# Two transformer blocks in one launch: the low half of every second early weight unit made by an accumulating transfer

## The chip, the cores and the metric

One Trainium2 chip, one core. The metric is the device time of one execution in microseconds (us); lower is better. TensorE multiplies, VectorE (DVE) and ScalarE (ACT) do elementwise work, GpSimd (POOL) does a little of it, SyncE (SP) issues the loads.

## The reference

The reference runs a block of a first model (a hybrid mixer, cross attention to a memory, a gated feed-forward) and then two layers of a second one, on one sequence of 512 positions and width 1024, in float32. What matters here is its beginning:

```python
h = x
hn = rmsnorm(h, norm_mix_g[l])
h = h + hybrid_mixer(hn, w_in[l], ...)            # z = hn @ w_in; three branches; concat @ w_out
hn = rmsnorm(h, norm_x_g[l])
mn = rmsnorm(mem, norm_mem_g[l])                  # 256 rows of memory
h = h + cross_attention(hn, mn, w_xq[l], w_xkv[l], w_xo[l])
```

`hybrid_mixer` projects `hn` by `w_in`, and has a spatially gated branch, a branch with a causal depthwise convolution of 31 taps, and a chunkwise mLSTM branch of four heads, each with its own q, k and v weights.

## The kernel before, in words

**Products.** TensorE multiplies in a float32 form of reduced precision (`fp32r`). Each operand is therefore split into a high half (rounded to that form) and a low half (the rest), and `mm` (from line 597) makes each product of three matmuls: high by high, high by low, low by high.

**Weights.** They come in units of 128 partitions by 1024 float32 values (512 KB). `wunit` (line 630) takes a raw tile `wr` (three buffers), a page `wh` for the high half and one `wl` for the low one, issues the load on SP's queue, and splits the unit in two column halves of 512. For each, `split` (line 614) has ACT copy the raw values into `wh` and VectorE subtract: `wl = wr - wh`. The unit of a head's q, k and v weights is 384 wide and has one such half.

**Order.** Nothing runs when the code calls it. Engine calls are recorded as steps by `Recorder`; `Plan` gives each a price (`price1` and `price`, lines 150 and 203, with the delay until another engine sees the result), computes priorities, and simulates list scheduling (`run`) with limited buffers; `improve` repeats this with priorities from the last plan, eight times, and keeps the plan that is shortest by its own prices. `emit` then issues all steps in the planned order, so that each engine works through a fixed sequence, with waits only where data or buffers demand them. All of these instructions carry the line of `emit`'s call, L509, in the profile; the rows are told apart by their tiles. Three more rules matter:

- A unit's load waits until the unit `quota` places earlier (5 here) has been used up, and for a free raw tile. A load without predecessors may be planned at most 60 us of TensorE work ahead.
- Where the plan leaves TensorE idle for over 1 us, `emit` fills the gap with matmuls of the identity against itself (`ps<-ident`), in a number fixed by the plan.
- A tile is free, in the plan, when its last step has ended.

**The first stages.** `mix` (line 861) makes 20 units: in the order of the code, four of `w_in` each for the mLSTM input, the convolution branch, the gated branch and the output gate, and four units of q, k, v weights. `mem` (line 1225) has eight units of `w_xkv` for the keys and eight for the values, and `w_out` has eight. Units of `mix` and the keys are used by `proj_t` or a loop like it (24 matmuls a unit; 512 columns wide for the mixer, 256 for the keys). The convolution's 31 taps for each of two channel blocks (`taps`, tiles `gcv`) run on VectorE, as do normalisations by many tiny steps (`sm`). Cross attention (`xattn`) and all that follows come after `w_out`.

Of the kernel before, what the change touches and what calls it, by code (L numbers as in the profile page):

```python
# [7 lines left out]
F32 = mybir.dt.float32  # L8
# [3 lines left out]
AF = mybir.ActivationFunctionType  # L12
OP = mybir.AluOpType
# [76 lines left out]
class Engine:  # L90
    def __init__(self, rec, name):
        self.rec, self.name = rec, name
# [5 lines left out]
class Recorder:  # L98
# [10 lines left out]
    def add(self, forms, bias=0.0):  # L109

        if self.held is not None:
            self.held += forms[0]
            return
        o = Op()
        o.i = len(self.ops)
        o.reads, o.writes, o.keep = [], [], self.keep
        for eng, method, args, kw in forms[0]:
            outs = [kw["out"] if "out" in kw else args[0]]
            if kw.get("accum_out") is not None:
                outs.append(kw["accum_out"])  # L120
            ins = [x for x in (args if "out" in kw else args[1:]) if is_ap(x)]
            ins += [x for k, x in kw.items() if k not in ("out", "accum_out") and is_ap(x)]
            for x in outs + ins:
                if on_chip(x):
                    self.tiles[x.tensor.name] = x.tensor
            o.writes += [region(x) for x in outs if on_chip(x)]
            o.reads += [region(x) for x in ins if on_chip(x)]
        o.forms = [(f[0][0], f) + price(f) + (bias if f[0][0] == "vector" else 0.0, port(f)) for f in forms]
        self.ops.append(o)
        return o  # L130
# [19 lines left out]
def price1(eng, m, args, kw):  # L150
    out = kw["out"] if "out" in kw else args[0]
    ins = [x for x in list(args[1:]) + [x for k, x in kw.items() if k not in ("out", "accum_out")] if is_ap(x)]
    n = width(out)
    if m == "dma_start":
        return n * 4 * int(out.shape[0]) / 360e3 * (1 if run(out) >= 128 else 2)
    if eng == "tensor":
        if m == "transpose":
            return 0.109
        if "float32r" in str(args[1].dtype):
            return max(n / 2285.0 + 0.007, width(args[1]) / 1200.0 + 0.0025)  # L160
        return 4 * max(n, 64) / 2400.0
    ps = any("PSUM" in str(x.space) for x in ins + [out])
    if eng == "scalar":
        aps = sum(1 for k in ("scale", "bias") if is_ap(kw.get(k)))
        return (0.052 if ps else 0.094) + n / 1200.0 + 0.093 * (aps + (kw.get("accum_out") is not None))
    if eng == "vector":
        if m in ("bn_stats", "tensor_reduce"):
            return 0.065 + width(ins[0]) / 960.0
        if m == "bn_aggr":
            return 0.075  # L170
        cols = sum(1 for x in ins[1:] if int(x.shape[-1]) == 1 and n > 1)
        if m in ("tensor_scalar", "tensor_copy"):
            if ps:
                return 0.125 + n / 960.0
            return 0.06 + n / 1920.0 + (0.065 * max(1, cols) if m == "tensor_scalar" else 0)
        if m == "scalar_tensor_tensor":
            return (0.13 if cols or ps else 0.065) + n / 960.0
        if m == "memset":
            return 0.05 + n / 1920.0
        return 0.068 + n / 960.0  # L180
    if m in ("memset", "affine_select"):
        return 0.1 + n / 1200.0
    if m == "tensor_scalar":
        return 0.22 + n / 960.0
    return 0.15 + n / 476.0
# [17 lines left out]
def price(calls):  # L203

    t = sum(price1(*c) for c in calls)
    eng = calls[0][0]
    return t, {"tensor": 0.22, "scalar": 0.16, "vector": 0.12, "gpsimd": 0.12, "sync": 0.9}[eng]


# [323 lines left out]
class Block:  # L533
    def __init__(self, ctx, tc, a, out):
        self.tc, self.a, self.out = tc, a, out
        self.nc = Recorder(tc.nc)
        self.n = 0
        E = ctx.enter_context
        self.const = E(tc.tile_pool(name="const", bufs=1))
        self.wp = E(tc.tile_pool(name="wp", bufs=N_RAW))  # L540
        self.pgp = E(tc.tile_pool(name="pgp", bufs=N_PAGE))
        self.s2p = E(tc.tile_pool(name="s2p", bufs=N_HALF))
        self.small = E(tc.tile_pool(name="small", bufs=1))
        self.psp = E(tc.tile_pool(name="psp", bufs=8, space=PSUM))
        self.rules(5)
        self.early = 0
        self.x = self.const.tile([P, NT, D], F32, name="x")

    def uid(self, s):
# [80 lines left out]
    def wunit(self, loads, n=1024):  # L630

        nc = self.nc
        raw = self.wp.tile([P, 1024], F32, tag="wr", name=self.uid("wr"))
        hi, lo = self.page("wh"), self.page("wl")
        firsts = []
        for view, src in loads:
            firsts.append(len(nc.ops))
            nc.sync.dma_start(view(raw), src)
        nc.units.append((firsts, hi.tensor.name, self.quota))
        for c in ((0, 512), (512, n)) if n > 512 else ((0, n),):  # L640
            self.split(hi[:, c[0]:c[1]], lo[:, c[0]:c[1]], raw[:, c[0]:c[1]], weights=True)
        return Split(hi, lo)

    def unit_t(self, w, c0):
# [215 lines left out]

    def mix(self):
        nc, a = self.nc, self.a
        col = self.cols
        w_in = a["w_in"][0]
        self.rules(5)
# [11 lines left out]
        for c in range(2):  # L877
            hi, lo, src = gu[:, :, 32 * c:32 * c + 4], gu[:, :, 64 + 32 * c:68 + 32 * c], gw[:, :, 4 * c:4 * c + 4]
# [383 lines left out]

    def xattn(self, xT, kT, vv):
        nc, a = self.nc, self.a
        w_q = a["w_xq"][0]
        self.rules(6)
        self.early = 5
        oT = []
        for h in range(4):
            q = []  # L1270
            for j in range(2):
                ps = self.proj_t(self.unit_t(w_q, (2 * h + j) * P), xT)
                q.append(self.pair("q"))
                self.split(q[j].hi, q[j].lo, ps, 1.0 / 16.0)
            pT = self.duo("pT")
            for i2 in range(2):
                ps = self.ps()
                for ii in range(2):
                    i = i2 * 2 + ii
                    for j in range(2):  # L1280
                        self.mm(ps[:, ii * 256:(ii + 1) * 256], q[j][:, i * P:(i + 1) * P], kT[2 * h + j],
                                j == 0, j == 1)
                nm = self.sm([P, 2])
                nc.vector.tensor_reduce(nm, ps.rearrange("p (h m) -> p h m", m=256), axis=AX.X, op=OP.max,
                                        negate=True)
                p = self.s2("p")
                sm = self.sm([P, 2])
                for ii in range(2):
                    c = slice(ii * 256, (ii + 1) * 256)
                    nc.scalar.activation(p[:, c], ps[:, c], AF.Exp, bias=nm[:, ii:ii + 1], accum_out=sm[:, ii:ii + 1])  # L1290
                nc.vector.reciprocal(sm, sm)
                for ii in range(2):
                    c = slice(ii * 256, (ii + 1) * 256)
                    nc.vector.tensor_scalar(p[:, c], p[:, c], sm[:, ii:ii + 1], None, op0=OP.mult)
                pt = self.ps()
                self.turn(pt, [p[:, ii * 256 + c * P:ii * 256 + (c + 1) * P] for c in range(2) for ii in range(2)])
                o = pT.both[:, :, i2 * 256:(i2 + 1) * 256]
                self.split(o.hi, o.lo, pt.rearrange("p (c t) -> p c t", t=256))
            for j in range(2):
                b = 2 * h + j  # L1300
                ps = self.ps()
                for m in range(2):
                    self.mm(ps, vv[m][b // 4][:, (b % 4) * P:(b % 4 + 1) * P], pT.blocks[m], m == 0, m == 1)
                o = self.pair("o")
                self.split(o.hi, o.lo, ps)
                oT.append(o)
            if h == 1:
                self.proj_n(oT, a["w_xo"][0], 0)
        return self.proj_n_steps(oT[4:], a["w_xo"][0], 512)
# [585 lines left out]
```

## Time and profile before

| | us |
|---|---|
| median of 3 runs | 1964.94 (1964.29 to 1970.25) |
| the profiled execution, its own time | 1964.42 |
| its span, first to last instruction | 1962.6 |
| granted TensorE clock, mean | 0.994 |

The profile is of one execution. A row of the page's groups gives the engine, the operation, out<-in by tile names, count, busy time, mean duration and the idle time of the engine just before. Engines pipeline, so a row's mean can exceed the distance between two such instructions. Times of the timeline and of the chain are counted from the start of the span.

### The profile page before, as it was taken

The numbers are of one execution on the slowest core, as the hardware profiler recorded it, in microseconds if no ns is written. First come the engines' busy times: TensorE is split into PE (matmuls) and PEld (weight loads), VectorE is DVE, ScalarE is ACT, GpSimd is POOL, SyncE is SP. The second block draws the span as 40 slices with busy tenths as digits, with TensorE's granted clock in tenths as the row PEclk, the third lists the DMA queues.
The fourth block names the chain that finished last, engine by engine and source line by source line (L and its number), as shares of the span: only waits on it lengthen the run. The fifth ranks groups of instructions, "written<-read, shape, count | busy, mean of one in ns | idle before, by whom it ended". The sixth has DMA issues, their size and how long they took to land.

```text
span 1962.6 us, 26913 instructions
## 1 busy us (share of the span) xinstructions
PE 1930.5 (98%) x10348; PEld 1645.3 (84%) x10348; DVE 1214.9 (62%) x2690; ACT 824.2 (42%) x1673; POOL 78.5 (4%) x123
## 2 busy tenths in 40 slices
PE   9999999999999999999999999999999999999998
PEld 8888889798888878988788888778998988888776
DVE  5999665565434457688884345347686775344356
ACT  5476534344322333576534233233575434223330
POOL 0021000000000000012200000000000000000001
PEclk9999999999999999999999999999999999999999
DMA  6222423323222433510332233243223322233241
GB/s 172 80 69 65 155 87 103 97 65 118 65 76 75 118 108 83 110 32 22 99 106 76 75 108 97 75 127 104 76 76 97 98 76 91 67 98 105 70 150 43
DMA packets 215466, 177.38 MB, mean 90 GB/s; under 512 B 25174, under 2 KB 194202, under 8 KB 215338
## 3 DMA queue, kind: packets, MB, share of 16 engines
q1 hardware_dynamic: 215338, 175.66, 30.6%
q8 instruction: 81, 1.33, 0.3%
q14 instruction: 47, 0.39, 0.1%
HBM read 173.54 MB, written 2.10 MB: 89 GB/s over the span
## 4 chain that ended last, share of the span: by engine, by line
PE 86%; DVE 9%; ACT 3%; DMA 2%; issue 1%; SPq 0%; POOL 0%; DVEq 0%; ACTq 0%
PE ps L509 86%; DVE wl L509 2%; DVE sm L509 1%; DVE gcv L509 1%; ACT wh L509 1%; ACT p L509 1%; DMA wr<-in_mlp_w_dram 1%; DVE xtl L509 0%; DVE x L509 0%; DVE pt L509 0%; DMA wr<-in_w_up_dram 0%; ACT xth L509 0%; DMA g<-in_norm_mix_g_dram 0%; DMA wr<-in_w_down_dram 0%; DMA wr<-in_a_w_out_dram 0%
## 5 line engine op out<-in xcount | busy, mean ns | idle before, releaser
L509 ACT ACTIVATE wh<-wr 128x512 fp32r<-128x512 f32 x625 | 357.1, 623 | 423.5 <-PE ps L509 271.5
L509 DVE TENSOR_TENSOR wl<-wr,wh 128x512 fp32r<-128x512 f32 x625 | 406.2, 686 | 205.6 <-PE ps L509 96.8
L509 PE MATMUL ps<-xth,wh 128*128 128x512 f32 (+1 forms) x1464 | 516.9, 353 | 0.4 <-ACT hg L509 0.4
L509 PE MATMUL ps<-xtl,wh 128*128 128x512 f32 (+1 forms) x1464 | 514.4, 351 | 1.4 <-DVE xtl L509 1.4
L509 PE MATMUL ps<-xth,wl 128*128 128x512 f32 (+1 forms) x1464 | 513.4, 351 | 0.0
L509 PE MATMUL ps<-wh,hid 128*128 128x512 f32 (+1 forms) x1392 | 436.4, 391 | 1.8 <-ACT wh L509 1.7
L509 PEld LDWEIGHTS ps<-wh,hid 128*128 128x128 f32 x1392 | 260.3, 188 | 61.6 <-ACT wh L509 3.3
L509 PEld LDWEIGHTS ps<-xtl,wh 128*128 128x128 f32 x1464 | 276.2, 189 | 41.4 <-DVE xtl L509 2.6
L509 PEld LDWEIGHTS ps<-xth,wh 128*128 128x128 f32 x1464 | 276.4, 189 | 40.2 <-ACT xth L509 0.8
L509 PEld LDWEIGHTS ps<-xth,wl 128*128 128x128 f32 x1464 | 275.7, 188 | 39.9 <-DVE wl L509 0.2
L509 PE MATMUL ps<-wl,hid 128*128 128x512 f32 (+1 forms) x696 | 272.4, 391 | 1.6 <-DVE wl L509 1.5
L509 DVE TENSOR_TENSOR x<-x,ps 128x512 f32<-128x512 f32 (+1 forms) x210 | 141.1, 678 | 162.8 <-PE ps L509 162.2
L509 PEld LDWEIGHTS ps<-wl,hid 128*128 128x128 f32 x696 | 130.8, 188 | 34.2 <-DVE wl L509 4.8
L509 DVE TENSOR_TENSOR r<-r 128x512 f32<-128x512 f32 x62 | 42.8, 691 | 99.8 <-ACT r L509 99.7
L509 PE MATMUL ps<-wl,xth 128*128 128x256 f32 (+2 forms) x320 | 94.4, 295 | 3.4 <-DVE wl L509 3.4
L509 PE MATMUL ps<-wh,xth 128*128 128x256 f32 (+2 forms) x320 | 94.7, 296 | 0.0
L509 PE MATMUL ps<-wh,xtl 128*128 128x256 f32 (+2 forms) x320 | 93.9, 293 | 0.0
L509 ACT ACTIVATE r<-ps 128x512 f32<-128x512 f32 x64 | 38.0, 593 | 114.9 <-PE ps L509 114.9
L509 DVE SCALAR_TENSOR_TENSOR cv<-ps,cols,cv 128x511 f32<-128x511 f32 (+2 forms) x56 | 41.8, 746 | 39.1 <-ACT cv L509 38.5
L509 PEld LDWEIGHTS ps<-wl,xth 128*128 128x128 f32 x320 | 60.4, 189 | 5.6 <-DVE wl L509 4.2
L509 PE MATMUL ps<-wh,o 128*128 128x512 f32 x192 | 62.3, 394 | 0.0
L509 PEld LDWEIGHTS ps<-wh,xth 128*128 128x128 f32 x320 | 60.3, 189 | 1.4
(352 smaller groups left out, 2438.9 us busy)
## 6 DMA issues: line engine op xcount, KB each, us to landing
wr<-in_mlp_w_dram SPq DMA_DIRECT2D x128, 512.0 KB, 4.2
wr<-in_w_up_dram SPq DMA_DIRECT2D x44, 512.0 KB, 3.9
wr<-in_c_w_in_dram SPq DMA_DIRECT2D x24, 512.0 KB, 3.8
wr<-in_w_down_dram SPq DMA_DIRECT2D x22, 512.0 KB, 3.6
wr<-in_w_in_dram SPq DMA_DIRECT2D x16, 512.0 KB, 4.3
wr<-in_w_xkv_dram SPq DMA_DIRECT2D x16, 512.0 KB, 3.8
wr<-in_w_out_dram SPq DMA_DIRECT2D x8, 512.0 KB, 4.5
wr<-in_w_xq_dram SPq DMA_DIRECT2D x8, 512.0 KB
```

The lines of the kernel that those rows point to most:

```text
L509: getattr(getattr(self.rec.nc, eng), method)(*args, **kw)
```

## The change

In the mixer, the memory projection and `w_out` (`self.adding` is on from `mix` until `xattn`), every second unit, by the count of units made so far, gets its low half in another way. ACT still copies raw into the high half; ACT then copies the high half, negated, into the low half; and once both column halves are so filled, one transfer issued on GpSimd's queue adds the raw tile onto the low half in place (`accum_op=OP.add`). VectorE's subtractions of those units are gone. The planner gets a price for such a transfer: 1.2 us on GpSimd's queue, and 3.5 us more until another engine sees the result.

```diff
@@ price
     t = sum(price1(*c) for c in calls)
     eng = calls[0][0]
+    if eng == "gpsimd" and calls[0][1] == "dma_start":
+        return 1.2, 3.5
     return t, {"tensor": 0.22, "scalar": 0.16, "vector": 0.12, "gpsimd": 0.12, "sync": 0.9}[eng]
@@ Block.__init__
         self.early = 0
+        self.adding = False
@@ Block.wunit
         nc.units.append((firsts, hi.tensor.name, self.quota))
+        add = self.adding and len(nc.units) % 2 == 0
         for c in ((0, 512), (512, n)) if n > 512 else ((0, n),):
-            self.split(hi[:, c[0]:c[1]], lo[:, c[0]:c[1]], raw[:, c[0]:c[1]], weights=True)
+            c = slice(*c)
+            if add:
+                nc.scalar.activation(hi[:, c], raw[:, c], AF.Copy)
+                nc.scalar.activation(lo[:, c], hi[:, c].bitcast(F32), AF.Copy, scale=-1.0)
+            else:
+                self.split(hi[:, c], lo[:, c], raw[:, c], weights=True)
+        if add:
+            nc.gpsimd.dma_start(out=lo[:, :n], in_=raw[:, :n], accum_op=OP.add)
         return Split(hi, lo)
@@ Block.mix
+        self.adding = True
@@ Block.xattn
+        self.adding = False
```

## Rows read from the trace of the kernel before

**Rows 1.** the page: its busy line, and the share of each engine in the chain that ended last.

```profile
PE 1930.5 (98%) x10348; PEld 1645.3 (84%) x10348; DVE 1214.9 (62%) x2690; ACT 824.2 (42%) x1673; POOL 78.5 (4%) x123
...
PE 86%; DVE 9%; ACT 3%; DMA 2%; issue 1%; SPq 0%; POOL 0%; DVEq 0%; ACTq 0%
```

**Rows 2.** busy time of each engine in six of the eight stretches up to 283 us (the columns are in the first line; in brackets the instructions).

```profile
core 0: us, PE busy (x) PEld busy (x) DVE busy (x) ACT busy (x) POOL busy (x), PEclk, DMA share, GB/s
...
10.90:28.70 17.80, 17.73 (x131) 16.14 (x130) 17.75 (x54) 14.18 (x36) 0.69 (x2) 1.00 0.81 206
...
47.50:123.00 75.50, 74.26 (x366) 60.89 (x365) 73.03 (x140) 41.62 (x71) 5.76 (x12) 1.00 0.26 76
123.00:144.50 21.50, 21.40 (x109) 18.32 (x110) 21.16 (x68) 16.82 (x34) 4.49 (x7) 0.92 0.19 50
144.50:163.60 19.10, 17.58 (x92) 14.54 (x91) 16.67 (x85) 8.73 (x19) 3.56 (x6) 0.91 0.29 83
163.60:195.50 31.90, 31.86 (x190) 27.96 (x191) 30.87 (x136) 23.01 (x44) 4.42 (x4) 1.00 0.22 67
195.50:283.00 87.50, 87.50 (x469) 74.72 (x468) 54.91 (x133) 35.91 (x75) 0.00 (x0) 1.00 0.38 121
```

**Rows 3.** TensorE: the costliest groups between 47.5 and 195.5 us by line (count, busy us, mean ns, idle before), and one piece of its timeline (start us, us, what).

```profile
L509 PE MATMUL ps<-ident 128*128 128x512 f32 x141 | 35.1, 406 | 0.0
L509 PE MATMUL ps<-xth,wh 128*128 128x512 f32 x56 | 22.9, 409 | 0.4 <-ACT hg L509 0.4
...
80.20 15.94 PE L509 MATMUL ps<-ident 128*128 128x512 f32 x69
```

**Rows 4.** the chain that ended last, in order of time (start us, us, what).

```profile
20.66 0.76 DVE nat L509
21.46 49.43 PE ps L509 x340
70.92 0.60 ACT xc L509
...
84.36 4.53 DVE gcv L509 x7
...
123.10 21.41 PE ps L509 x107
...
145.07 0.74 DVE pw L509 x2
...
163.64 119.28 PE ps L509 x654
```

**Rows 5.** the page's group of the low weight halves (count, busy us, mean ns, idle before).

```profile
L509 DVE TENSOR_TENSOR wl<-wr,wh 128x512 fp32r<-128x512 f32 x625 | 406.2, 686 | 205.6 <-PE ps L509 96.8
```

**Rows 6.** VectorE's timeline: pairs of low halves.

```profile
77.82 1.28 DVE L509 TENSOR_TENSOR wl<-wr,wh 128x512 fp32r<-128x512 f32 x2
...
117.02 2.39 DVE L509 TENSOR_TENSOR wl<-wr,wh 128x512 fp32r<-128x512 f32 x2
```

**Rows 7.** the same stretches for the instructions that write or read `wl` alone (engines TensorE, its weight loads, VectorE).

```profile
47.50:123.00 75.50, 25.38 (x67) 12.41 (x66) 11.25 (x16) 1.00 0.26 76
123.00:144.50 21.50, 8.43 (x22) 4.48 (x22) 3.17 (x5) 0.92 0.19 50
144.50:163.60 19.10, 4.15 (x12) 2.26 (x12) 2.63 (x4) 0.91 0.29 83
163.60:195.50 31.90, 8.64 (x27) 5.10 (x27) 3.82 (x6) 1.00 0.22 67
195.50:283.00 87.50, 51.00 (x144) 26.95 (x143) 25.83 (x40) 1.00 0.38 121
```

**Rows 8.** VectorE's timeline before the first weights are used.

```profile
17.31 0.69 DVE L509 TENSOR_TENSOR wl<-wr,wh 128x512 fp32r<-128x512 f32 x1
...
19.72 0.68 DVE L509 TENSOR_TENSOR wl<-wr,wh 128x512 fp32r<-128x512 f32 x1
```

**Rows 9.** ScalarE's timeline: a pair of high halves.

```profile
54.40 1.15 ACT L509 ACTIVATE wh<-wr 128x512 fp32r<-128x512 f32 x2
```

**Rows 10.** transfers: from issue to landing of all loads into `wr`, and two kinds of load up to 300 us (count, KB each, median us to landing).

```profile
DMA to landing us min/median/max: 3.1/4.0/9.6
...
wr<-in_w_in_dram SPq DMA_DIRECT2D x16, 512.0 KB, 4.3
...
wr<-in_w_q_c_dram SPq DMA_DIRECT2D x4, 64.0 KB, 3.6
```

**Rows 11.** GpSimd's timeline: the subtraction beside the slow pair of rows 6.

```profile
117.51 1.35 POOL L509 TENSOR_TENSOR pl<-pw,ph 128x512 fp32r<-128x512 f32 x1 [1.28 <-ACT ph L509]
```

**Rows 12.** SP's queue: what it waited for up to 300 us, two loads of the key projection (one lies between them), and issue to landing of the loads from 180 to 256 us.

```profile
SPq L509 <- DVE wl L509: 185.3, 40, 19.1
...
197.50 0.34 SPq L509 DMA_DIRECT2D wr<-in_w_xkv_dram  x1
...
203.18 0.33 SPq L509 DMA_DIRECT2D wr<-in_w_xkv_dram  x1
...
DMA to landing us min/median/max: 3.7/3.9/4.5
```

**Rows 13.** TensorE's timeline near the dip of the granted clock (a bracket is idle time before, and its releaser).

```profile
120.73 0.39 PE L509 MATMUL ps<-v,ph 128*128 128x258 f32 x1 [0.54 <-DVE pw L509]
...
125.93 0.63 PE L509 MATMUL ps<-xth,wl 128*128 128x512 f32 x1
```

## The prediction, made before the changed kernel was run

> **What bounds the kernel now.** I began with the busy line and the chain over the whole span: TensorE is busy 98% of it and carries 86% of the chain that ended last, VectorE 9% [rows 1]. That says little about the edit, because TensorE's share holds filler. The change touches only the mixer, the memory projection and `w_out`, so the table by stretch comes next. It is cut where the chain changes hands, up to 283 us, where `w_out` is done [rows 2]. From 195.5 to 283 us VectorE has room (busy 54.91 of 87.5 us). From 47.5 to 195.5 us it has next to none: 73.03 of 75.5, 21.16 of 21.5, 16.67 of 19.1 and 30.87 of 31.9 us. TensorE looks full there too, but the lines of that stretch show 141 matmuls of `ident` against itself, the planner's filler, in runs such as 69 in 15.94 us, or 0.23 us apiece: some 32 us without real work [rows 3]. The chain in order of time agrees: from 70.92 to 123.10 us it is VectorE with short gaps, and again from 145.07 to 155.29 us, mostly the convolution's taps (`gcv`) and small statistics, with weight halves (`wl`) between them [rows 4]. After 163.64 us it reads as TensorE, but filler is part of that. So in this stage the end is set by VectorE's backlog, and every VectorE microsecond taken out before 195.5 us can become less filler. After 283 us nothing is edited, and I count no change there.
>
> **What leaves VectorE.** Every second unit counted in the order of the code: ten of the mixer's 20 (three are the narrow `qkv` ones), eight of the memory's 16, four of `w_out`'s eight, 22 in all. A half of 128x512 costs VectorE 0.686 us as a mean [rows 5], and two in a row take 1.28 us [rows 6], so about 0.60 us each when packed; all 22 units are 41 subtractions, some 24 us. Only those in the bound stretch count. The table of `wl` by stretch gives 16, 5, 4 and 6 between 47.5 and 195.5 us, 31 together [rows 7]. Half of them are 15.5, times 0.60 us = 9.3 us. The 40 from 195.5 us on are worth nothing: TensorE runs there almost without filler and covers them. Before 28.7 us VectorE is also full (17.75 of 17.8 us [rows 2]); the four halves at 17.31 to 20.32 us stand on the way to the last `nat`, after which TensorE starts on the weights at 21.46 us [rows 4, 8]. Unit 2 is one of these two units, so 2 x 0.60 = 1.2 us. Gain: 10.5 us.
>
> **What ACT takes on.** A negated copy per half; two copies `wh<-wr` take 1.15 us [rows 9]. The mixer's ten units and the memory's first three make 23 copies, some 13 us over the whole front, and 15.5 x 0.52 = 8 us inside the bound stretch, where ACT is busy 41.62 + 16.82 + 8.73 + 23.01 = 90.2 of 148 us [rows 2]. It rises to about two thirds, and I cost it at nothing while ACT has such gaps. Where it is ahead of an `xth` or `hg` on ACT's queue, TensorE already waits 0.4 us once [rows 3]; with the cover gone at all 23 that would be 9 us, which belongs to the wide end of the range.
>
> **What the transfer costs.** GpSimd issues no transfer in this trace, so its time T, from the start on that queue to the landing, is bounded. Below: the fastest weight load, 3.1 us from issue to landing. Above: the slowest, 9.6 us [rows 10]. Size hardly matters in these rows: 64 KB lands in 3.6 us and 512 KB in 4.3 us, so the bytes themselves are about 0.7 us of it. The new transfer reads a second stream, which I price as another 0.7 us, and its issue on GpSimd at 1.35 us, the longest single GpSimd subtraction [rows 11]: T = 4.0 (the median) + 0.7 + 1.35 = 6.0 us. This is nearest to an ordinary load, because it is one with more on it. The planner's new price, 1.2 + 3.5 us, is below that by 1.3 us. The plan also calls the raw tile free 1.2 us after the issue, although it is being read until the landing.
>
> The DMA page of the Trainium skill (DMA: Bandwidth & Descriptors, Anatomy of one DMA) fits a GpSimd-issued transfer as 2.0 us plus bytes over 436 GB/s; with the destination read too that would be an estimated 4.4 us here, and the loss of the next paragraph would be nought.
>
> **Where lateness bites.** There are three raw tiles, and SP's queue waited 185.3 us for `wl` to give them back [rows 12]. While keys are projected, loads follow each other by 2.84 us (two of them lie 5.68 us apart, from 197.50 us [rows 12]); that I take for TensorE's pace of one unit, since TensorE is busy throughout [rows 2]. An ordinary raw tile needs 3.9 us to land [rows 12], 1.2 for the copies and 0.6 for the trailing subtraction, 5.7 us; a new one 3.9 + 1.2 + 1.2 + T = 6.3 + T. Three tiles pass two units in (12.0 + T)/3 us, one in 2.0 + T/6. At T = 6.0 this is 3.0 us, 0.16 over that pace. Of the 16 units some five are prefetched (the quota), so 11 x 0.16 = 1.8 us is lost. At T = 3.1 it is nothing; at 9.6 it is 11 x 0.76 = 8.4 us. Queued behind a waiting load on SP are only later loads; behind a waiting transfer on GpSimd are the mask selects of `pw` and the `pl` subtractions, whose reader is TensorE. In the mixer a unit on TensorE takes 24 matmuls at 0.23 us = 5.5 us, so units are read well ahead and I cost lateness there at nothing; uncovered, each of its ten would add up to T. `w_out`'s units also last 5.5 us each and stay covered.
>
> **Sum.** -9.3 - 1.2 + 1.8 = -8.7 us on the profiled execution's own 1964.42 us (span 1962.6 us and 1.8 us around it): 1955.7 us. The median of the runs, 1964.94 us, stands 0.5 us above that execution, so 1956.2 us.
>
> **Rivals.**
> *The relief is absorbed.* All orders come out of a list planner that runs afresh, and VectorE's long chains (31 taps for each of two blocks, normalisations in series) need not get shorter when the gaps between them do. For it: the chain holds 21.41 us of TensorE in mid-stretch [rows 4]. Against it: VectorE has no idle time to speak of there. Then the gain is 0 to 5 us: about 1962 us.
> *Raw tiles are held too long.* The point is the key and value projection from 197.5 us. Break-even with 10.5 us of gain is 11 x (T/6 - 0.84) = 10.5, that is T = 10.8 us; if ACT's copies delay TensorE by 5 us, T = 8 us is enough. At T = 14 us it loses 16.4 - 10.5 = 6 us: 1971 us. A stall of TensorE is dearer than its length: after gaps like that at 120.73 us [rows 13] the granted clock of 123 to 163.6 us was 0.91 to 0.92 [rows 2], and a matmul of 512 columns took 0.63 us against a mean of 0.41 [rows 3, 13]: for part of it the clock was at 1.2 in place of 2.4 GHz.
> *The transfer starves beside VectorE.* At 117.02 us a `wl` pair took 2.39 us in place of 1.28 while GpSimd subtracted [rows 6, 11], so the two engines do block each other. If the making of a transfer's descriptors on GpSimd waits likewise for VectorE, which does not rest, each of the 13 early transfers gains several such 1.1 us, T passes 10 us, and TensorE waits in the mixer: 13 x 2 - 10.5 is 15.5 us slower, some 1980 us. For it: the collision. Against it: it has been seen with both engines reading.
> The SBUF page of the Trainium skill (SBUF — State Buffer, Who interferes with whom) says a GpSimd-issued transfer starves under VectorE's two-port forms (copies, `tensor_scalar`), and infers that `tensor_tensor` spares it; by this the rival would be confined to a few small operations, and no run here shows it yet.
> *It hardly does what it says*: if the planner moves the new units' work out of the full stretch, nothing changes; this is part of the first rival.
>
> **How the numbers follow.** Forecast 0.45; absorbed 0.30; raw tiles 0.17; starved 0.08. About 0.3% (5.9 us) is what a measurement of this kernel can tell from no change. The forecast's own spread (T from 3.1 to 9.6: -10.5 to -2 us) puts a tenth of the chance inside that bound, and the first rival can give a little more than 5 us when the new plan packs well: faster 0.42, same 0.34, slower 0.24. The range goes from 1948 us (all 41 subtractions' worth near the front, less a third) to 1974 us, where raw tiles are held at T = 9.6 us and the relief is absorbed; with a starved transfer left out, that is about 8 in 10.
>
> **What would show it.** Right: 41 fewer `wl` subtractions on VectorE; fewer than 141 filler matmuls before the keys, by some 35; `w_out` ending about 8 us earlier than 283 us; from there on the old profile, shifted. Wrong: waits of TensorE for `wl` landings, loads spaced over 3.2 us in the key projection, the transfer landing after 8 us or more, or a front with the same filler as now.

## The result, and the profile after

| | before | after |
|---|---|---|
| median, us (4 runs each) | 1964.62 (1960.54 to 1970.25) | 1987.2 (1985.89 to 1990.3) |
| the profiled execution, us | 1964.42 | 1985.89 |
| its span, us; mean granted clock | 1962.6; 0.994 | 1984.2; 0.993 |

The ratio is 1.0115, 95% interval 1.0087 to 1.0144: slower by 22.6 us, where 8.7 us of gain were forecast.

The page first: the busy line, the chain by engine, and the two DMA queues (packets, MB, share of 16 engines). They answer to [rows 1].

```profile
PE 1930.3 (97%) x10327; PEld 1642.7 (83%) x10327; DVE 1199.0 (60%) x2658; ACT 844.7 (43%) x1710; POOL 94.3 (5%) x141
...
q1 hardware_dynamic: 215338, 175.66, 30.3%
q0 software_dynamic: 3168, 10.55, 3.0%
...
PE 78%; DVE 9%; DMA 6%; ACT 5%; issue 2%; POOL 0%; SPq 0%; DVEq 0%; POOLq 0%; ACTq 0%
```

TensorE's busy time is that of before (1930.3 against 1930.5 us), so the 21.6 us of the longer span are idle time of TensorE (what the busy time lost in filler it got back in slower matmuls, where the clock fell). Its share of the chain fell from 86% to 78%; DMA rose from 2% to 6% and ACT from 3% to 5%. A queue that was not there before, GpSimd's, moved 10.55 MB.

The table by stretch is cut as [rows 2] are, with the filler's group of 47.5 to 195.5 us below it (as in [rows 3]).

```profile
core 0: us, PE busy (x) PEld busy (x) DVE busy (x) ACT busy (x) POOL busy (x), PEclk, DMA share, GB/s
10.90:28.70 17.80, 14.35 (x92) 12.54 (x93) 13.54 (x47) 11.09 (x32) 0.86 (x1) 0.90 0.89 208
47.50:123.00 75.50, 72.19 (x375) 59.71 (x374) 66.69 (x127) 43.63 (x71) 6.74 (x12) 1.00 0.46 111
123.00:144.50 21.50, 21.38 (x106) 17.60 (x105) 20.61 (x72) 17.42 (x38) 6.24 (x11) 1.00 0.09 26
144.50:163.60 19.10, 16.97 (x95) 13.67 (x95) 16.04 (x68) 12.18 (x28) 1.33 (x2) 1.00 0.52 115
163.60:195.50 31.90, 29.79 (x181) 25.77 (x181) 29.65 (x110) 25.77 (x49) 8.67 (x12) 1.00 0.47 121
195.50:283.00 87.50, 73.23 (x382) 61.52 (x381) 37.49 (x126) 40.76 (x80) 7.78 (x9) 0.92 0.63 162
```

```profile
L511 PE MATMUL ps<-ident 128*128 128x512 f32 x116 | 27.5, 393 | 0.0
```

Two things are to be seen. Between 47.5 and 195.5 us VectorE did lose work: 133.0 us busy against 141.7, and TensorE got 116 filler matmuls in place of 141. But in the last row TensorE is busy 73.23 of 87.5 us where it had been busy throughout, and the DMA engines' share is 0.63 where it was 0.38. The startup row has the same sign: TensorE 14.35 of 17.8 us, against 17.73.

Next, the same front by three marks of TensorE: the last start of its matmuls of the first `w_in` units (`xth` by `wl`, 256 columns), the first of the key projection (`mt` by `wh`), and the last of `w_out` (`wh` by `yc`):

| | `w_in` part | keys begin | `w_out` ends | keys to `w_out` |
|---|---|---|---|---|
| before | 46.6 | 189.0 | 282.1 | 93.1 |
| after | 52.4 | 190.5 | 309.0 | 118.5 |

The startup loses 5.8 us, the mixer regains 4.3, and then keys, values and `w_out` lose 25.4. Behind that the rest of the kernel is some 5 us shorter (1675.2 against 1680.5 us).

What TensorE waited for in that stage is in the chain in order of time (start us, us, what):

```profile
205.97 5.48 DMA wr<-in_w_xkv_dram
...
211.52 2.69 issue
214.22 7.14 DMA wl<-wr
...
221.42 4.47 DMA wr<-in_w_xkv_dram
225.92 0.64 ACT wh L511
...
238.46 4.77 DMA wr<-in_w_xkv_dram
...
245.98 4.63 DMA wl<-wr
...
251.09 6.10 DMA wr<-in_w_out_dram
...
259.75 4.54 DMA wl<-wr
...
264.35 4.96 DMA wr<-in_w_out_dram
...
285.56 6.39 DMA wl<-wr
```

Read it as a loop. A transfer that reads a raw tile lands after 7.14 us, at 221.36 us; the tile is free then, and SP, which had issued nothing since 214.22 us, issues the next load into it at 221.42; that takes 4.47 us; ACT copies the high half; and TensorE starts at last, as its timeline shows (a bracket is idle time before, and its releaser):

```profile
214.30 0.36 PE L511 MATMUL ps<-mt,wl 128*128 128x256 f32 x1 [1.48 <-DMA wl<-wr]
...
219.61 0.50 PE L511 MATMUL ps<-wh,mt 128*128 128x512 f32 x1 [2.06 <-ACT wh L511]
...
226.60 0.50 PE L511 MATMUL ps<-wh,mt 128*128 128x512 f32 x1 [3.15 <-ACT wh L511]
```

The profile names ACT, which is the last link; the transfer two links back is the one that was late. The loads of the chain landed in 4.5 to 6.1 us, against 3.9 us at the median before [rows 12]. Two pieces of 10 us of that stage, with the columns of the table by stretch, show the DMA engines at a share of 0.90 and 0.98:

```profile
205.00:215.00 10.00, 8.52 (x73) 8.35 (x72) 1.76 (x4) 4.48 (x10) 1.62 (x2) 1.00 0.90 211
215.00:225.00 10.00, 6.16 (x33) 4.93 (x31) 2.05 (x4) 3.88 (x8) 0.93 (x2) 0.83 0.98 217
```

The transfers themselves (KB each, median us from start to landing; then the landing times of all 22; then, on GpSimd, the time of the issue in ns, minimum, median and maximum):

```profile
wl<-wr POOLq DMA_DIRECT2D x19, 512.0 KB, 5.2
...
wl<-wr POOLq DMA_DIRECT2D x3, 192.0 KB, 3.2
```

```profile
DMA to landing us min/median/max: 3.0/5.2/8.2
```

```profile
L511 POOL DMA_DIRECT2D wl<-wr x22: 850/860/1045, 7.7 to 285.6; - x22
```

So T, which the prediction set at 6.0 us, was 5.2. The 3.0 us is a unit of 192 KB; the fastest of 512 KB took 4.5, and the 8.2 is the first transfer of the kernel. And what the two queues took of the DMA engines between 190 and 283 us:

```profile
q1 hardware_dynamic: 5568, 10.49, 35.4%
q0 software_dynamic: 1296, 4.72, 27.4%
```

10.49 MB are 20 loads of 512 KB; 35.4% of 93 us are 32.9 us of all sixteen engines, 1.65 us a load. The kernel before has the same figures in that stretch:

```profile
q1 hardware_dynamic: 6464, 10.49, 35.4%
```

Of the second queue, 4.72 MB are nine transfers; 27.4% are 25.5 us, 2.83 us a transfer. An accumulating transfer holds the engines 1.7 times as long as a load of its size. By these figures two units of the key projection used to need 3.3 us of the engines in the 5.68 us that TensorE takes for them [rows 12], and now need 6.1 (two loads and one transfer).

### The profile page after: what moved, and what is told of

Same layout as the page of the kernel before. It is cut to its first block, busy times and chain, and to the rows that moved or that the text cites. A ratio compares the mean times of both kernels' runs of the same rounds, so it can differ in the third digit from the quotient of the medians.

```text
span 1984.2 us, 26944 instructions
## 1 busy us (share of the span) xinstructions
PE 1930.3 (97%) x10327; PEld 1642.7 (83%) x10327; DVE 1199.0 (60%) x2658; ACT 844.7 (43%) x1710; POOL 94.3 (5%) x141
## 3 DMA queue, kind: packets, MB, share of 16 engines
q0 software_dynamic: 3168, 10.55, 3.0%
## 4 chain that ended last, share of the span: by engine, by line
PE 78%; DVE 9%; DMA 6%; ACT 5%; issue 2%; POOL 0%; SPq 0%; DVEq 0%; POOLq 0%; ACTq 0%
PE ps L511 78%; DVE wl L511 2%; DMA wl<-wr 2%; DVE sm L511 1%; ACT wh L511 1%; DVE gcv L511 1%; DMA wr<-in_w_in_dram 1%; DMA wr<-in_w_xkv_dram 1%; DMA wr<-in_mlp_w_dram 1%; ACT L511 1%; ACT p L511 1%; DMA wr<-in_w_out_dram 1%; DVE x L511 0%; DVE pt L511 0%; DVE xtl L511 0%
## 5 line engine op out<-in xcount | busy, mean ns | idle before, releaser
L511 DVE TENSOR_TENSOR wl<-wr,wh 128x512 fp32r<-128x512 f32 x584 | 381.5, 690 | 206.3 <-ACT wh L511 102.6
L511 PE MATMUL ps<-wh,xth 128*128 128x256 f32 (+2 forms) x320 | 94.7, 296 | 1.0 <-ACT wh L511 1.0
```

What stands on the lines that cost most here:

```text
L511: getattr(getattr(self.rec.nc, eng), method)(*args, **kw)
```

## The experiments

The theory after the result: the relief is there, and the transfer takes it back and more, through (a) its bytes on the DMA engines that the loads use, (b) the raw tile that it holds until it lands, (c) the low half that is late. The rivals: the relief itself was absorbed; GpSimd's issue or the starved transfer; the plan, which was made with other prices. The first six kernels keep the changed kernel's plan and the order of every queue, and replace only what is issued for each transfer when the plan is written out.

**1. The transfer left out** (below: the stub). In its place GpSimd adds one column.

```diff
+                    if eng == "gpsimd" and method == "dma_start":
+                        lo, raw = kw["out"], kw["in_"]
+                        self.rec.nc.gpsimd.tensor_add(lo[:, 0:1], raw[:, 0:1], lo[:, 0:1].bitcast(F32))
+                        continue
```

> The changed kernel's own plan and queue order on every engine, but each of the 22 accumulating transfers is replaced at its place on GpSimd's queue by an addition of one column (the sum is left out: the low halves hold only the negated high halves beyond that column). So the raw tile comes free and the low half is ready about 6 us earlier per unit; ACT's 41 negated copies and the re-made plan stay. Theory A (the time is lost because a raw tile is held until the transfer has landed, so that loads in SP's queue and then ACT and TensorE wait): back to 1952 to 1966 us. Rival C (ACT's 41 extra copies in its queue cost the time) and rival D (the plan came out worse whatever the transfer takes): 1980 us or more.

Measured: 1955.28 us, 0.9951 [0.9936, 0.9966], 9.7 us under before. The relief is not absorbed; the change's plan is a good one while nothing waits for the transfer, and the transfer costs 32 us on it.

**2. 16 columns, which nobody reads,** and **3. the whole transfer, which nobody reads.** Both add the high half onto a scratch in HBM (the sum is left out):

```diff
+                        kw = dict(kw, out=self.scratch[self.at, :, :k], in_=self.high[kw["out"].tensor.name].bitcast(F32))
```

with k = 16 columns (the source cut alike), and with k the unit's width.

> The changed kernel's plan and queue order, but each transfer adds 16 columns of the high half onto a scratch in HBM that nobody reads (the sum is left out): the same number of transfers and descriptors, 1/64 of the bytes. Beside the stub (1955.3 us) and the full-size transfer onto the scratch (1967.2 us): if the moved bytes cost the 12 us, this is within 3 us of the stub, 1955 to 1958 us, and the loads of the key and value projection land in some 4.0 us again; if issue, descriptors and a transfer's fixed time cost it, it stays at 1964 to 1968 us.

> The changed kernel's own plan and queue order; each transfer has the same size, queue and place, but adds the high half onto a scratch tensor in HBM that nobody reads (the sum on the low half is left out). Raw tile and low half are both free of it, so only the traffic and GpSimd's issue time stay. Theory A (hold and lateness): 1953 to 1961 us, near the run without the transfer (1955.3). Rival E (the transfers' traffic slows the weight loads, and that is the loss): 1970 us or more.

Measured: 1955.11 us, 0.9941 [0.9926, 0.9956], with 16 columns; 1967.16 us, 1.0009 [0.9999, 1.0020], with all. Issue, descriptors and the fixed time of 22 transfers cost nothing that can be told from the stub. The bytes, with no one waiting for the sum, cost up to 12 us, which lies between the two expectations, and take the whole relief. Between 190 and 283 us the scratch transfers held the engines as the real ones did (ten of them 30.4% of 93 us, again 2.83 us each):

```profile
scratch<-wh POOLq DMA_DIRECT2D x10, 512.0 KB, 8.5
```

```profile
q1 hardware_dynamic: 7504, 11.01, 36.8%
q0 software_dynamic: 1440, 5.24, 30.4%
```

A destination in HBM makes each land later (8.5 us), and the pages of high halves are held till then; how much of the 12 us is that, and how much slower loads, was not told apart.

**4. 16 columns of the real transfer.** Raw onto low half, as in the change, the rest of the sum left out:

```diff
+                        kw = dict(kw, out=kw["out"][:, :16], in_=kw["in_"][:, :16])
```

> The changed kernel's plan and queue order, but each transfer adds only the first 16 columns of raw onto the low half (the rest of the sum is left out): raw tile and low half wait for the transfer as in the change, for its fixed time only. If the bytes are what makes the transfer long and the loads late, T falls from 5.2 to some 3 us and the time from 1987 to about 1965 to 1970 us; if the fixed time and the order of the queues are what costs, T stays over 4 us and the time over 1978 us.

Measured: 1959.31 us, 0.9962 [0.9947, 0.9976], better than either expectation. From 190 to 283 us, its transfers, its queues and, in the stretch of the table above, its engines:

```profile
wl<-wr POOLq DMA_DIRECT2D x10, 8.0 KB, 3.2
```

```profile
q1 hardware_dynamic: 6464, 10.49, 35.4%
q0 software_dynamic: 1440, 0.08, 2.7%
```

```profile
195.50:283.00 87.50, 84.42 (x429) 70.08 (x428) 44.73 (x114) 44.47 (x92) 7.76 (x9) 1.00 0.41 122
```

All waits of the change are in this kernel: the raw tile is held and the low half is late, for 2.0 to 5.7 us (2.4 at the median, over the whole front):

```profile
DMA to landing us min/median/max: 2.0/2.4/5.7
```

They cost 4 us beside the stub. So 28 of the transfer's 32 us hang on its bytes: on what these hold of the engines, and on the longer time that tile and low half then wait. A trap of the view of waits: SP's queue, up to 283 us, waited for these transfers almost as long as it did in the change,

```profile
SPq L513 <- DMA wl<-wr: 84.0, 18, 13.2
```

```profile
SPq L511 <- DMA wl<-wr: 94.2, 19, 13.3
```

the first being this kernel, the second the change; yet 28 us lie between them. A queue of prefetches waits most of the time, for whatever comes last; the length of that wait says nothing of its price.

**5. Late low half alone,** and **6. held raw tile alone.** The transfer adds the high half in place of raw onto the low half, so that raw is free after ACT's copies; or it adds the high half onto the raw tile in place, so that the tile is held and the low half is ready early. Either way the sum with raw is left out:

```diff
+                        kw = dict(kw, in_=self.high[kw["out"].tensor.name].bitcast(F32))
```
```diff
+                        kw = dict(kw, out=kw["in_"], in_=self.high[kw["out"].tensor.name].bitcast(F32))
```

> The changed kernel's own plan and queue order; each transfer adds the high half, not the raw tile, onto the low half (so the low halves come out as zero). Same bytes and same place in the queues: the low half is ready as late as in the changed kernel, but the raw tile is free after ACT's copy. Theory A1 (the held raw tile costs the time): 1954 to 1966 us. Theory A2 (the late low half, on which TensorE waits, costs it): 1975 to 1988 us.

> The mirror of e8: the same plan and order; each transfer adds the high half onto the raw tile in place (so the low halves hold only the negated high halves). The raw tile stays taken until the transfer has landed, but the low half is ready after ACT's negated copy. A1: 1974 to 1988 us. A2: 1954 to 1966 us. If e8 and e9 each lose some 10 us, both count.

Measured: 1972.92 us, 1.0047 [1.0030, 1.0064], and 1980.21 us, 1.0081 [1.0064, 1.0098]. The first lies between its two expectations, the second in the range of a costly held tile. With the same bytes as the 1967.2 us of run 3 (though these land in SBUF), lateness adds some 6 us, the held tile some 13, and both together, which is the change, 20. The signatures are a direct wait of TensorE in the one, and SP's wait for the tile in the other (up to 330 and up to 300 us):

```profile
PE ps L514 <- DMA wl<-wh: 9.0, 6, 3.7
```

```profile
SPq L514 <- DMA wr<-wh: 94.7, 20, 15.9
```

The set, by the marks of the table above (us). The marks are of one profiled execution each; its own time stands beside the median, and is 4.9 us below it in run 3 and 7.0 above it in run 5:

| same plan, same order | `w_in` part | keys begin | keys to `w_out` | profiled | median |
|---|---|---|---|---|---|
| left out (1) | 47.3 | 183.1 | 94.6 | 1956.9 | 1955.3 |
| 16 columns, nobody reads (2) | 47.6 | 181.8 | 94.7 | 1956.4 | 1955.1 |
| 16 columns, real (4) | 47.2 | 181.4 | 99.0 | 1959.6 | 1959.3 |
| all, nobody reads (3) | 51.4 | 185.7 | 99.4 | 1962.3 | 1967.2 |
| late low half alone (5) | 51.3 | 190.0 | 106.4 | 1979.9 | 1972.9 |
| held tile alone (6) | 51.3 | 188.3 | 110.2 | 1979.1 | 1980.2 |
| the change | 52.4 | 190.5 | 118.5 | 1985.9 | 1987.2 |

With plan and order the same, the startup loss comes with the bytes: 47.2 to 47.6 without them, 51.3 to 52.4 with them, whoever reads the sum.

**7. Mixer alone,** and **8. memory and `w_out` alone** (`adding` turned off, or on, at the memory projection):

```diff
         w_kv = a["w_xkv"][0]
+        self.adding = False
```

> New units in the mixer alone (10 of 22); the memory projection and w_out split as before. Theory A places 25 of the 22 to 27 us lost in the stretch of keys, values and w_out, where TensorE needs a unit every 2.8 us: here that loss should go, 1958 to 1968 us. Rival D (a worse plan in the front): 1975 us or more.

> New units in the memory projection and w_out alone (12 of 22). Theory A: 1980 to 1992 us, as the changed kernel. Rival D: within 6 us of the kernel before.

Measured: 1962.35 us, 0.9985 [0.9975, 0.9995], with the mixer's ten units; 1980.6 us, 1.0081 [1.0063, 1.0099], with the other twelve. The loss is made by the units of memory and `w_out`, the gain by the mixer's. The two together, -2.6 and +15.6, leave 9.6 us of the 22.6 to the combination.

**9. A plan that knows.** The planner is told that a transfer's tiles are taken until it lands, and that it lands 5.0 us after its 1.2 us on GpSimd's queue, in place of 3.5; the rest is the change.

```diff
-        return 1.2, 3.5
+        return 1.2, 5.0
...
-                last[t] = max(last.get(t, 0.0), end)
+                hold = lat if e == "gpsimd" and calls[0][1] == "dma_start" else 0.0
+                last[t] = max(last.get(t, 0.0), end + hold)
```

> The change as it is, but the planner is told that the raw tile (and the low half's buffer) stays taken until the transfer has landed, 5.0 us after its 1.2 us on GpSimd's queue, in place of 1.2 us; the landing delay goes from 3.5 to 5.0 us. Theory A in its physical form (three raw tiles can't pass the units faster, however they are ordered): 1977 to 1990 us. Rival B (the plan ordered SP's and ACT's queues for a tile that isn't free, so that each waits in the wrong place; an honest plan recovers it): 1960 to 1970 us.

Measured: 1972.49 us, 1.0041 [1.0026, 1.0056]. That lies between the two expectations, and almost 15 of the 32 us are gone. The change's own plan orders work as if the raw tile came free 1.2 us after the issue, which is the likely reason; but a plan made anew differs in every queue, and how far the time moves by that alone was not measured (run 12 below went the other way). The 15 us do not add to the 28 that hang on the bytes: in run 4, with the same false price but a short transfer, all waits cost only 4 us. The bytes stay, and so do slow loads; up to 330 us:

```profile
wl<-wr POOLq DMA_DIRECT2D x19, 512.0 KB, 5.3
wr<-in_w_xkv_dram SPq DMA_DIRECT2D x16, 512.0 KB, 5.4
wr<-in_w_out_dram SPq DMA_DIRECT2D x8, 512.0 KB, 5.6
```

where the kernel before has 3.8 and 4.5 us for those two loads.

**10 to 12. A fourth raw tile** (one page less for it): the change, the kernel before as its control, and the change with the plan of run 9.

```diff
-    N_PAGE = 33
+    N_PAGE = 32
-    N_RAW = 3
+    N_RAW = 4
```

> The change with four raw tiles in place of three and 32 pages in place of 33. A1: a unit may be held a third longer, so most of the loss goes, 1958 to 1972 us. A2: 1980 us or more.

> The kernel before with four raw tiles and 32 pages: the control for the two runs with four tiles. Theory A: within 6 us of the kernel before, since its loads wait for a raw tile only where TensorE is ahead of need.

> All 22 new units, four raw tiles (32 pages), and the planner told that tile and buffer are taken for 5.0 us after the issue. If the four tiles did not help before because the plan handed them out too early, they should now: 1962 to 1970 us. If the late low half is what is left, as with three tiles: 1970 to 1976 us.

Measured: 1982.83 us, 1.0091 [1.0074, 1.0108]; 1970.62 us, 1.0026 [1.0016, 1.0037]; 1990.59 us, 1.0126 [1.0108, 1.0145]. The control shows that a raw tile more and a page less, with the plan made for them, cost 5 us by themselves: its `w_out` ends at 278.7 us, 3.4 earlier than before, and what lies behind is 12 us longer. The change with four raw tiles is in the range that was expected if the late low half were the cost; only beside its control, where it costs 12 us in place of 22.6, does the held tile show again, by another route. The last run is a miss, 18 us slower than run 9 with its three tiles, and 8 us slower than run 10, which has the false price. Of the 15.1 us between the profiled executions of runs 9 and 12, 9.1 lie behind `w_out`, where the control lost too; `w_out` itself ends at 297.9 us in place of 291.9, and why the front is these 6 us longer stays open.

**13. Added from HBM.** The transfer reads the weights from HBM again, so no raw tile is held:

```diff
-            nc.gpsimd.dma_start(out=lo[:, :n], in_=raw[:, :n], accum_op=OP.add)
+            for view, s in loads:
+                nc.gpsimd.dma_start(out=view(lo), in_=s, accum_op=OP.add)
```

> The change in full, but the transfer adds the weights from HBM, read a second time, instead of from the raw tile, which is then free (in the plan and on the chip) as soon as ACT has made the high half, earlier than in the kernel before. The plan is re-made for it. A1: 1952 to 1966 us. A2: 1970 to 1988 us, since the low half comes as late as in the change (or later: pieces of 512 bytes for units laid out by columns).

Measured: 1977.61 us, 1.0060 [1.0043, 1.0077]. The tile is free, but the transfers are slower, 9.1 us for units of `w_xkv`, 8.5 for `w_in`, 6.5 for `w_out`, and TensorE waits for them.

**14. The mixer alone, with the plan that knows** (the edits of runs 7 and 9):

> New units in the mixer alone, and the planner told of the hold. VectorE's relief of some 6 to 9 us in the mixer should come out where units are read 5.5 us apart: 1955 to 1962 us, faster than the kernel before by more than the run with the mixer alone (1962.4). If lateness in the mixer takes the relief back whatever the plan knows: 1961 to 1967 us.

Measured: 1953.93 us, 0.9942 [0.9926, 0.9958]. This beats both kernels, by 11 us the one before, and is just under the range expected. Its first `w_in` units end at 50.8 us, 4.2 later than before, so the startup loss stays; its keys begin at 181.7 us, 7.3 earlier, and its `w_out` ends at 273.9. Up to 330 us its transfers take a share of the engines of 7.4%, against 17.8% in the change, and from 195.5 us on, where none is issued, TensorE is as good as full:

```profile
q0 software_dynamic: 1440, 4.26, 7.4%
```

```profile
195.50:283.00 87.50, 86.63 (x455) 73.12 (x454) 60.78 (x161) 41.96 (x88) 0.00 (x0) 1.00 0.40 126
```

The same ten units without that plan (run 7) gave 1962.35 us, 8 us more; here too one plan stands against one other.

## Why the prediction was wrong

**The bound and the relief: right, but for the startup.** Forecast were -10.5 us with the transfer at nothing; the stub measured -9.7. VectorE lost 8.7 us of work in the bound stretch (9.3 forecast), 41 subtractions went, and the filler fell by 25 matmuls and 7.6 us (35 matmuls forecast). The 1.2 us of the startup were not there: in the stub the first `w_in` units end 0.7 us later than before. That term came from a misread chain. It took 21.46 us for TensorE's start on the weights, but before the change TensorE multiplies with `wl` from 16.5 us on, and has hardly a gap up to 28.7 us (busy 17.73 of 17.8 us [rows 2]). Those matmuls are in this line (count, ns, first and last start):

```profile
L509 PE MATMUL ps<-xth,wl x80: 274/281/288, 16.5 to 46.6; 128*128 128x256 f32 x80
```

Of the stub's profiled gain of 7.4 us in span, 5.9 are in hand when the keys begin; 1.5 are given back by the end of `w_out`, and 3.0 come after it, where the sum had none.

**ACT's copies at nothing: right.** ACT is busy 99.0 us in the bound stretch in place of 90.2, 8.8 more where 8 were forecast, and the stub, which has all these copies, keeps the whole gain.

**T: right.** 5.2 us at the median against 6.0, with 0.86 us of issue against 1.35. The estimate from the DMA page of the Trainium skill (DMA: Bandwidth & Descriptors, Anatomy of one DMA) was 4.4 us; transfers of 512 KB took 4.5 us at the fastest (259.75 us in the chain above) and 5.2 at the median, so it fits the fastest and not the middle. Shrunk to 8 KB the transfer took 2.0 us at the least and 2.4 at the median, and the least agrees with the 2.0 us of fixed time that this page of the Trainium skill gives.

**Where lateness bites: the step that failed.** It priced the transfer at 11 x 0.16 = 1.8 us; the runs show 32. The pace 2.0 + T/6 with the measured T of 5.2 us would have given 2.87 us and 0.3 us of loss, so T was not at fault. Nor is a longer load enough: with the 5.4 us of run 9 in place of 3.9 the same sum gives 20.2 / 6 = 3.37 us a unit, an estimated 6 us of loss, where keys to `w_out` took 23.9 us longer than in the stub. The sum lets three tiles pass units without any of them waiting for its place in a queue. Three things that the step went by were wrong:

- *The bytes.* From 64 KB in 3.6 us and 512 KB in 4.3 [rows 10] the prediction read "the bytes themselves are about 0.7 us", and entered the load at 3.9 us whatever else moved. These are landing times on engines that were not full. The slowest load of the same rows, 9.6 us, was issued in the first 12 us, where the engines' share was high (0.81 from 10.9 to 28.7 us [rows 2]); of those issued later, none that the trace times took over 4.5 us. The prediction took the 9.6 as an upper bound of T, and not as a load's time on full engines. What the engines are held for is 1.65 us a load and 2.83 us a transfer, and the 1.65 was to be had before the change, from the share of the load queue over its bytes. With a transfer in every second unit the engines need 6.1 us in each 5.68; between 205 and 225 us their share was 0.90 and 0.98, and the loads of the chain landed in 4.5 to 6.1 us, one of its transfers in 7.14. The DMA page of the Trainium skill (DMA: Bandwidth & Descriptors, SWDGE vs HWDGE vs iDMA) says that transfers issued by GpSimd and by SP use the same sixteen engines, which take turns between their queues; the slower loads agree with that.
- *Covers that were taken for granted.* Lateness in the mixer at nothing and a startup that gains: the keys begin 7.4 us later than in the stub, and 5.1 of these are lost in the first `w_in` units, in a stretch where the DMA engines' share was 0.81 before the change [rows 2]. `w_out` "stays covered": from 251.09 us the chain waits for its loads and a transfer.
- *The plan.* The prediction saw that it calls a raw tile free 1.2 us after the issue, and gave that no price. The plan that knows takes back 15 us, though chance between two plans is not ruled out (run 9).

A further part, not separated, is the clock. Where TensorE waited, its granted clock fell to 0.83:

```profile
215.00:235.00 20.00, 14.34 (x71) 11.89 (x70) 8.48 (x32) 10.04 (x22) 0.93 (x2) 0.83 0.70 185
235.00:255.00 20.00, 19.20 (x84) 14.82 (x82) 8.77 (x25) 9.51 (x18) 2.58 (x3) 1.00 0.79 188
255.00:275.00 20.00, 13.67 (x44) 10.42 (x45) 4.26 (x7) 9.06 (x17) 1.72 (x2) 0.83 0.75 207
```

A mean of 0.83 is a third of the time at 1.2 in place of 2.4 GHz: by that estimate some 13 us of the 40 in the first and the last row. In run 4 the clock is 1.00 in that stage. The prediction named this dearness of a stall, in a rival only.

**The rivals.** *Raw tiles are held too long* had the place and the mechanism, and run 6 shows it as the largest single wait; but its condition, T over 10.8 us, was not met, for it used the same formula. *The relief is absorbed* falls by run 1, which keeps 9.7 us of it. *The transfer starves beside VectorE* falls: the issue on GpSimd took 0.85 to 1.05 us in all 22, although VectorE was busy some nine tenths of the bound stretch, and 8 KB landed in 2.4 us on the same order of instructions. The SBUF page of the Trainium skill (SBUF — State Buffer, Who interferes with whom) infers that `tensor_tensor` spares such transfers; that agrees.

**What stays open.** The 12 us of the bytes that nobody reads are not split into slower loads and held pages; why four raw tiles do not go with the plan that knows is not explained; why the rest of the kernel, behind `w_out`, is 3.0 us shorter in the stub and 5.3 in the change was not looked into; and how much two plans of the same work differ by chance was not measured.

## What to carry to other kernels

Cost a new transfer twice: by its time to land, and by what it holds of the DMA engines, which is its queue's share of the engines times the stretch over the number of transfers; then add that to what the loads of the same stage hold already. Moving work to a transfer pays in a stage where the engines have room (here the mixer: 2.6 us with the change's prices, 11 with the plan that knows) and not where each unit's load is used as it lands. And a planner that is given a new kind of step should know for how long that step holds its tiles: here the plan that did was 8 us faster on the mixer and 15 us on the whole change, but 8 us slower with four raw tiles, so the new plan has to be measured too.

## What the runs showed of the hardware that was not expected

- An accumulating transfer of 512 KB from SBUF to SBUF held the sixteen engines for 2.83 us, a load of 512 KB from HBM for 1.65 us. With HBM as the destination it held them as long, but landed after 8.5 us in place of 5.5 (medians, 190 to 283 us); with HBM as the source the medians were 6.5 to 9.1 us.
- Of the 5.2 us to landing, the median over the whole front, only 2.4 are left at 8 KB. In the rows of plain loads the difference between 64 and 512 KB had been 0.7 us [rows 10].
